# How x is loaded in a batched two-layer expert kernel: x(0) to x(3) in four loads from SyncE, x(4) to x(7) in one cast load from GpSimd

## The chip, the core and the metric

One core of a Trainium2 chip runs the kernel. The core has five engines: TensorE (PE) multiplies matrices, VectorE (DVE) and ScalarE (ACT) work on rows of data, GpSimd (POOL) and SyncE (SP) mostly issue transfers here. Sixteen DMA engines move data between HBM and the on-chip memory SBUF; matrix products come out in PSUM. Each program keeps its own order on each engine, and the engines meet through semaphores. The metric is the device time of one execution in microseconds (us), the median over runs.

## The reference

```python
n_experts, capacity, hidden, expert_hidden = 8, 256, 512, 2048
# x (8, 256, 512), w1 (8, 512, 2048), w2 (8, 2048, 512), all float32
h = np.matmul(x, w1)
h = np.maximum(h, 0)
return np.matmul(h, w2).astype(np.float32)
```

Eight independent experts, each with 256 rows of x, two matrix products and a ReLU between them. The weights are 67.1 MB in float32, x and the output 4.19 MB each.

## The kernel before

All sums are made in bfloat16 with float32 accumulation. The weights go from float32 in HBM to bfloat16 in SBUF inside the DMA (a cast load), which only GpSimd issues here. A weight slot w_sb holds one expert's w1 or w2 in bfloat16, and there are eight slots, so that two pairs of experts fit.

The experts run in four pairs p. For each pair GpSimd issues one load for both w1 and one for both w2 (4096 KB written each; for the last pair one load per expert, and its w2 in two pieces each). From the third pair on, such a load waits until PE has finished with the slots of two pairs earlier. GpSimd's loads go down one software ring, in order. SyncE counts their landings and hands PE a credit (t_w) for each.

x has to be transposed before it can be used. This is done for four experts at a time (a group g of two pairs): PE multiplies 128x128 blocks of the bfloat16 copy x_b with an identity into PSUM (ph), and ACT and DVE copy that into xt in the order in which the products need it (`untie`; who = 0 is ACT, who = 1 is DVE). Then for each expert PE makes h in four steps of 512 columns of w1, ACT and DVE write the ReLU of it in turns to ht, and PE makes the output from ht and w2 in PSUM (po). ACT and DVE copy it to x_f, which serves as the output's buffer too, and SyncE stores it: three pairs in one store of 3072 KB, which it issues once the first piece of the last expert's w2 has landed, and the last two experts in one store of 512 KB each.

Where x comes from before the change: x(0) and x(4 to 7) are loaded as float32 into x_f by SyncE, on its hardware ring, with rows of 4 KB and 16 KB per partition. Both stand inside the frame: the program up to `tc.close()`, at the end of which all engines meet at a barrier (line 96 in the profile) before any goes on. GpSimd loads x(1) and x(2 to 3) behind the frame as cast loads straight into x_b, ahead of all weights. ACT casts x(0) from x_f to x_b at the start; ACT and DVE cast one half each of x(4 to 7) during pair 0, when PE no longer reads the first group from x_b. SyncE waits for GpSimd's two x loads (line 145) and counts them for PE (t_x).

The lines that the change touches, by the profile's numbers: L91 the x loads, L145 SyncE's wait for them, L181 the casts, L192 and L196 the copies of `untie` for the first group, L287 the transposes.

Of the kernel before, what the change touches and what calls it, by code (L numbers as in the profile page):

```python
# [9 lines left out]
def kernel(  # L10
# [13 lines left out]
    nc = tc.nc  # L24
    P = 128
    bf = mybir.dt.bfloat16
# [3 lines left out]
    E, C, H = x.shape  # L30
    F = w1.shape[2]
    MT = C // P
    KT1 = H // P
# [4 lines left out]
    NG = E // 4  # L38
    J = 4 * MT
# [8 lines left out]
    def x_rows(es):  # L48

        flat = x[es].rearrange("e c k -> (e c k)")  # L50
        return flat.rearrange("(p f) -> p f", p=P)

    def sbuf(name, shape, dtype):
        return nc.alloc_sbuf_tensor(name, (P, *shape), dtype)

    def sem(name):
        return nc.alloc_semaphore(name)
# [1 line left out]


    x_f = sbuf("x_f", (NG, J, H), f32)
    x_b = sbuf("x_b", (J, H), bf)
    xt = sbuf("xt", (KT1, MT, 4 * P), bf)

    w_sb = sbuf("w_sb", (8, F * KT1), bf)
# [2 lines left out]
    ph = nc.alloc_psum_tensor("pt_h", (P, 2, FB, C), f32)  # L68
    po = nc.alloc_psum_tensor("pt_o", (P, 2 * MT, H), f32)

    s_x = [sem(f"s_x{i}") for i in range(4)]
    s_w = [sem(f"s_w{i}") for i in range(8)]
    s_cut = [sem(f"s_cut{b}") for b in range(2)]
    s_id = sem("s_id")
# [1 line left out]
    s_pe = sem("s_pe")  # L76
    t_x = sem("t_x")
# [5 lines left out]

    LOADS = [(0, 1), (4, 8), (1, 2), (2, 4)]

    def load_x(eng, to, i):
        a, b = LOADS[i]
        dst = to[:, MT * (a % 4):MT * ((b - 1) % 4 + 1), :].rearrange("p j k -> p (j k)")  # L90
        return eng.dma_start(dst, x_rows(slice(a, b))).then_inc(s_x[i], 16)  # L91

    for i in (0, 1):
        tc.no_tile_sem_insts.add(load_x(nc.sync, x_f[:, LOADS[i][0] // 4], i).ins.name)
    tc.close()
    tc.compile()  # L96

# [2 lines left out]
    at_t = lambda g, k: base(2 * g) - KT1 + k + 1  # L102
# [5 lines left out]


    pool = nc.gpsimd  # L110
    for i in (2, 3):
        load_x(pool, x_b, i)
    place = lambda p, i, b: 4 * i + 2 * (p % 2) + b
    landed = []
    for p, i in [(p, i) for p in range(NP) for i in range(2)]:
        joint = p < NP - 1
        for b in range(0, 2, 1 + joint):
            e, n = 2 * p + b, 1 + joint
            if p > 1:
                last = b + n - 1  # L120
                pool.wait_ge(s_pe, at_o(p - 2, last) if i else at_h(p - 2, last, NQ - 1))
            src = (w2_r if i else w1_r)[e:e + n].rearrange("e p f -> p e f")
            to = place(p, i, b)
            dst = w_sb[:, to:to + n]
# [15 lines left out]


    sp = nc.sync
    for i in (2, 3):
        sp.wait_ge(s_x[i], 16)
    sp.sem_inc(t_x, 1)  # L145
    times = [0] * len(s_w)
    for to, i, n in landed:
        times[to] += 1
# [21 lines left out]
    for who, (eng, copy, act) in enumerate((  # L170
        (nc.scalar, nc.scalar.copy, lambda o, i: nc.scalar.activation(o, i, relu)),  # L171
        (nc.vector, nc.vector.tensor_copy, nc.vector.tensor_relu),
    )):
        def cast(g):
            if g:
                eng.wait_ge(s_pe, at_t(g - 1, KT1 - 1))

            n = J // 2 if g else MT
            j0 = who * n
            eng.wait_ge(s_x[g], 16)  # L180
            copy(x_b[:, j0:j0 + n, :], x_f[:, g, j0:j0 + n, :]).then_inc(t_x, 1)  # L181

        def untie(g):


            for k in range(who, KT1, 2):
                eng.wait_ge(s_pe, at_t(g, k))
                src = ph[:, k // 2].bitcast(bf).rearrange("p a b -> p (a b)")
                src = src[:, k % 2 * J * P:(k % 2 + 1) * J * P]
                one, two = xt[:, k, :, :2 * P], xt[:, k, :, 2 * P:]  # L190
                if g == 0:
                    copy(  # L192
                        one.rearrange("p m (eh r) -> p m eh r", eh=4),
                        src[:, :4 * P].rearrange("p (eh r m) -> p m eh r", eh=4, m=MT),
                    )
                    last = copy(  # L196
                        two.rearrange("p m (e h r) -> p m h e r", e=2, h=2),
                        src[:, 4 * P:].rearrange("p (m h e r) -> p m h e r", m=MT, h=2, e=2),
                    )
                    continue  # L200
                for i in range(2):
                    part = src[:, 4 * P * i:4 * P * (i + 1)].rearrange(
                        "p (m h q) -> p m h q", m=MT, h=2
                    )
                    copy(  # L205
                        one.rearrange("p m (e h r l) -> p l m h e r", e=2, h=2, l=2)[:, i],
                        part[:, :, :, :P // 2].rearrange("p m h (e r) -> p m h e r", e=2),
                    )
                last = copy(  # L209
                    two.rearrange("p m (q l) -> p l m q", l=4),  # L210
                    src.rearrange("p (l m q) -> p l m q", l=4, m=MT)[:, :, :, P // 2:],
                )
            last.then_inc(t_h[who], 1)

        if who == 0:
            cast(0)
        for p in range(NP):
            if p % 2 == 0:
                untie(p // 2)
            for b in range(2):  # L220
                for q in range(who, NQ, 2):
                    eng.wait_ge(s_pe, at_h(p, b, q))
                    act(ht[:, b, FB * q:FB * (q + 1), :], ph[:, q % 2]).then_inc(t_h[who], 1)  # L223
            if p % 2 == 0 and p // 2 + 1 < NG:
                cast(p // 2 + 1)
            for b in range(2):
                eng.wait_ge(s_pe, at_o(p, b))
                if p == NP - 1:
                    copy(res(p)[:, MT * b + who, :], po[:, 2 * b + who, :]).then_inc(s_fin[b], 1)  # L229
                    continue  # L230
                for h in range(2):
                    src = po[P // 2 * h:P // 2 * (h + 1), 2 * b + who, :]
                    last = copy(res(p)[P // 2 * b:P // 2 * (b + 1), 2 * who + h, :], src)  # L233
                last.then_inc(t_o, 1)
# [5 lines left out]
    def take(s, n):  # L240
        pe.sem_inc(s, -n).wait_op(s, n, "sem-ge")  # L241

    def counter(name, step):

        r = nc.alloc_registers(name, engines=PE)
        nc.regs_mov(r, 0)
        add = lambda n: nc.regs_alu(r, r, n, op=mybir.AluOpType.add)
        now = lambda most: nc.snap(
            r, engines=PE, min_val=0, max_val=most, guaranteed_mod_val=0, out_of_modulus=step
        )  # L250
        return add, now

    def at(t, part, moved, dtype, *dims):

        n = part + moved
        dims_in = "abc"[:len(t.shape) - 1]
        line = t[:].rearrange(f"p {' '.join(dims_in)} -> p ({' '.join(dims_in)})")
        size = 2 if dtype == bf else 4
        last = sum(step * (num - 1) for step, num in dims) + 1
        got = line.bitcast(mybir.dt.uint8)[:, bass.ds(n, last * size)].bitcast(dtype)  # L260
        return bass.AP(got.tensor, got.offset, [got.ap[0], *([a, b] for a, b in dims)])

    def ready(places, **how):

        for place in places:
            pe.lower_ap(place, **how)
        return places

    def weights(places):
        return ready(places, for_matmul_weights=True)  # L270
# [2 lines left out]
        pe.sem_inc(s, 1)  # L273
    pe.sem_inc(t_o, 4)
    pe.wait_ge(s_id, 2)
    with nc.Fori(0, NG, engines=PE):
        take(t_x, 2)
        for t in t_h:
            take(t, 1)
        add_k, now_k = counter("r_k", 2)  # L280
        add_p, now_p = counter("r_p", 2 * J * P)
        with nc.Fori(0, KT1, engines=PE):
            k_at, p_at = now_k(2 * (KT1 - 1)), now_p(2 * J * P * (KT1 - 1))
            dsts = ready([at(ph, 2 * P * j, p_at, bf, [1, P]) for j in range(J)])
            srcs = weights([at(x_b, 2 * H * j, k_at, bf, [KT1, P]) for j in range(J)])
            for dst, src in zip(dsts, srcs):
                mm = pe.transpose(dst, src, identity[:])  # L287
            mm.then_inc(s_pe, 1)
            add_k(2)
            add_p(2 * J * P)  # L290
        W = 2 * F * KT1
        add_x, now_x = counter("r_x", 2 * P)
        add_w, now_w = counter("r_w", 4 * FB)
# [3 lines left out]
        with nc.Fori(0, 2, engines=PE):  # L297
            add_h, now_h = counter("r_h", 2 * C)
            add_o, now_o = counter("r_o", 4 * H * MT)
            with nc.Fori(0, 2, engines=PE):  # L300
                take(t_w, 1)
                with nc.Fori(0, NQ // 2, engines=PE):
                    x_at, w_at = now_x(6 * P), now_w(3 * W + 4 * FB)
                    cols = ready([
# [15 lines left out]
                    add_w(4 * FB)  # L320
                add_w(W - 2 * FB * NQ)
                add_x(2 * P)
# [3 lines left out]
            def second(kt0, n, turns=1):  # L326
                top = kt0 + n * (turns - 1)
                h_at, w_at = now_h(2 * C * (KT2 + top)), now_2(2 * H * (3 * KT2 + top))
                steps = [(kt, mt) for kt in range(n) for mt in range(MT)]
                cols = ready([at(w_sb, 4 * W + 2 * H * kt, w_at, bf, [1, H]) for kt in range(n)])  # L330
                rows = weights([
# [52 lines left out]
```

## Time and profile before

| what | value |
|---|---|
| time, median of 3 runs | 179.06 us (178.99 to 179.12) |
| time of the profiled execution | 179.03 us |
| its span, first to last instruction | 177.7 us |
| PE busy | 127.3 us (72%) |
| DVE, ACT, POOL busy | 36.1, 34.5, 9.4 us |
| software ring (GpSimd's loads) | 34.34 MB written, 91.0% of 16 DMA engines' span |
| hardware ring (SyncE's transfers) | 6.82 MB written, 9.3% |
| HBM read and written | 71.30 MB and 4.19 MB |

The execution took 1.3 us more than its span, which lies around the first and last instruction. The two rings' shares are the time that their packets took, divided by 16 engines' span; a share over 1 in a stretch comes about where packets of one DMA engine overlap, or where more of them start in the stretch than end in it. Bytes of a cast load are counted as written, and its reads are twice that.

### The profile page before, as it was taken

Reading aid. Unit: us, or ns where it says so; the run is one execution under the profiler, and the core shown is the slowest. Engines: PE = TensorE matmul, PEld = TensorE weight load, DVE = VectorE, ACT = ScalarE, POOL = GpSimd, SP = SyncE. Lnnn points to the kernel's source line nnn. Section 1 sums busy time; section 2 is a strip of 40 time slices with the busy share of each in tenths; the row PEclk is TensorE's granted clock in tenths of the full one; section 3 lists DMA queues with packets and bytes.
Section 4 is the critical chain, followed back from the end, with each engine's and each line's share of the span. In section 5 each row is a group of like instructions: output and inputs, shape, how many; then the busy total and the mean of one; then the engine's idle time right before and its main releaser. Section 6 shows DMA issues by size and latency. Waiting matters only on the chain. (4 is left out here: it accounts for less than half of the span.)

```text
span 177.7 us, 2366 instructions
## 1 busy us (share of the span) xinstructions
PE 127.3 (72%) x832; PEld 90.0 (51%) x832; DVE 36.1 (20%) x41; ACT 34.5 (19%) x43; POOL 9.4 (5%) x20
## 2 busy tenths in 40 slices
PE   0008000599929992899959993599999999999960
PEld 0007000499813440699814453489944489964420
DVE  0002100022340203022310309123222034420110
ACT  4104000024410202024200209022402042220110
POOL 3600000000010001001000202000000000000000
PEclk9999999999996998589969999579999999999997
DMA  6999999999999999999999999999999999999998
GB/s 236 376 240 210 236 203 210 236 203 210 236 207 207 236 207 207 236 210 203 236 210 203 236 210 203 236 218 195 236 218 195 236 218 203 209 224 204 291 435 341
DMA packets 3760, 41.16 MB, mean 232 GB/s; under 512 B 304, under 2 KB 304, under 8 KB 1200
## 3 DMA queue, kind: packets, MB, share of 16 engines
q0 software_dynamic: 2784, 34.34, 91.0%
q1 hardware_dynamic: 976, 6.82, 9.3%
HBM read 71.30 MB, written 4.19 MB: 425 GB/s over the span
## 5 line engine op out<-in xcount | busy, mean ns | idle before, releaser
L315 PE MATMUL pt_h<-xt,w_sb 128*128 x512 | 62.9, 290 | 24.4 <-PEq L241 24.4
L315 PEld LDWEIGHTS pt_h<-xt,w_sb 128*128 x512 | 59.3, 147 | 28.2 <-issue 25.2
L335 PE MATMUL pt_o<-w_sb,ht 128*128 x256 | 59.4, 394 | 6.1 <-PEq L241 5.8
L335 PEld LDWEIGHTS pt_o<-w_sb,ht 128*128 x256 | 25.5, 101 | 38.8 <-issue 12.2
L223 DVE TENSOR_SCALAR ht<-pt_h 128x1024 bf16<-128x1024 f32 x16 | 19.6, 1224 | 65.2 <-PE pt_h L315 65.2
L171 ACT ACTIVATE ht<-pt_h 128x1024 bf16<-128x1024 f32 x16 | 16.4, 1024 | 62.1 <-PE pt_h L315 62.1
L233 DVE COPY x_f<-pt_o 64x512 f32<-64x512 f32 x12 | 8.3, 689 | 42.1 <-PE pt_o L335 42.0
L233 ACT COPY x_f<-pt_o 64x512 f32<-64x512 f32 x12 | 7.0, 581 | 47.9 <-PE pt_o L335 47.8
L287 PE MATMUL pt_h<-identity,x_b 128*128 128x128 bf16 x64 | 5.6, 264 | 14.0 <-PEq L241 14.0
L287 PEld LDWEIGHTS pt_h<-identity,x_b 128*128 x64 | 5.1, 128 | 14.3 <-issue 14.0
L130 POOL DMA_DIRECT2D w_sb<-in_w_dram x8 | 5.4, 675 | 79.1 <-PE pt_h L315 60.6
L192 DVE COPY xt<-pt_h 128x512 bf16<-128x512 bf16 x2 | 1.4, 692 | 16.6 <-PE pt_h L287 16.6
L229 ACT COPY x_f<-pt_o 128x512 f32<-128x512 f32 x2 | 1.2, 586 | 14.4 <-PE pt_o L335 14.4
L229 DVE COPY x_f<-pt_o 128x512 f32<-128x512 f32 x2 | 1.4, 692 | 12.4 <-PE pt_o L335 12.4
L192 ACT COPY xt<-pt_h 128x512 bf16<-128x512 bf16 x2 | 1.2, 586 | 10.7 <-PE pt_h L287 10.7
L181 ACT CAST x_b<-x_f 128x1024 bf16<-128x1024 f32 (+1 forms) x2 | 2.9, 1468 | 0.3 <-DMA x_f<-in_x_dram 0.3
L209 ACT COPY xt<-pt_h 128x512 bf16<-128x512 bf16 x2 | 2.7, 1328 | 0.0
L209 DVE COPY xt<-pt_h 128x512 bf16<-128x512 bf16 x2 | 2.6, 1276 | 0.0
L127 POOL DMA_DIRECT2D w_sb<-in_w_dram x2 | 1.1, 531 | 16.3 <-PE pt_o L335 16.3
L181 ACT ACT_TABLE_LOAD x1 | 1.3, 1283 | 2.4 <-PEq L96 2.4
L205 ACT COPY xt<-pt_h 128x256 bf16<-128x256 bf16 x4 | 1.6, 487 | 0.0
L205 DVE COPY xt<-pt_h 128x256 bf16<-128x256 bf16 x4 | 1.6, 442 | 0.0
(11 smaller groups left out, 6.4 us busy)
## 6 DMA issues: line engine op xcount, KB each, us to landing
w_sb<-in_w_dram POOLq DMA_DIRECT2D x6, 4096.0 KB, 60.8
w_sb<-in_w_dram POOLq DMA_DIRECT2D x2, 2048.0 KB, 58.2
out_dram<-x_f SPq DMA_DIRECT2D x1, 3072.0 KB, 11.0
w_sb<-in_w_dram POOLq DMA_DIRECT2D x2, 1280.0 KB, 56.1
x_f<-in_x_dram SPq DMA_DIRECT2D x1, 2048.0 KB, 8.4
w_sb<-in_w_dram POOLq DMA_DIRECT2D x2, 768.0 KB, 59.2
out_dram<-x_f SPq DMA_DIRECT2D x2, 512.0 KB, 6.8
x_f<-in_x_dram SPq DMA_DIRECT2D x1, 512.0 KB, 3.2
```

The costliest lines, as they stand in the source:

```text
L130: pool.dma_start(dst, src).then_inc(s_w[to], 16)
L171: (nc.scalar, nc.scalar.copy, lambda o, i: nc.scalar.activation(o, i, relu)),
L181: copy(x_b[:, j0:j0 + n, :], x_f[:, g, j0:j0 + n, :]).then_inc(t_x, 1)
L192: copy(one.rearrange("p m (eh r) -> p m eh r", eh=4), src[:, :4 * P].rearrange("p (eh r m) -> p m eh r", eh=4, m=MT),)
L205: copy(one.rearrange("p m (e h r l) -> p l m h e r", e=2, h=2, l=2)[:, i], part[:, :, :, :P // 2].rearrange("p m h (e r) -> p m h e r", e=2),)
L209: last = copy(two.rearrange("p m (q l) -> p l m q", l=4), src.rearrange("p (l m q) -> p l m q", l=4, m=MT)[:, :, :, P // 2:],)
L223: act(ht[:, b, FB * q:FB * (q + 1), :], ph[:, q % 2]).then_inc(t_h[who], 1)
L229: copy(res(p)[:, MT * b + who, :], po[:, 2 * b + who, :]).then_inc(s_fin[b], 1)
L233: last = copy(res(p)[P // 2 * b:P // 2 * (b + 1), 2 * who + h, :], src)
L287: mm = pe.transpose(dst, src, identity[:])
L315: mm = pe.matmul(ph[:, q, i, :], row, cols[kt], start=(kt == 0), stop=(kt == KT1 - 1),)
L335: mm = pe.matmul(outs[mt], row, cols[kt], start=(kt0 + kt == 0), stop=(kt0 + kt == KT2 - 1),)
```

## The change

x(0) to x(3) are loaded by SyncE as float32 into x_f, one load of 512 KB per expert with rows of 4 KB per partition, each with its own semaphore. The first stands in the frame, the other three directly behind it. x(4 to 7) come in one cast load of GpSimd, its first, into a second half of x_b, which is twice as large now. The casts of the first group are split over ACT (x(0), x(2)) and DVE (x(1), x(3)); the casts of the second group and SyncE's wait for x are gone, and ACT and DVE count x(4 to 7) for PE after the ReLUs of pair 0. `untie` of the first group is one copy per 128 rows of K where it was two, since the rows of its four experts now all lie alike. PE's counter r_k goes on into the second half of x_b.

```diff
-    x_b = sbuf("x_b", (J, H), bf)
+    x_b = sbuf("x_b", (NG, J, H), bf)
...
-    LOADS = [(0, 1), (4, 8), (1, 2), (2, 4)]
-
-    def load_x(eng, to, i):
-        a, b = LOADS[i]
-        dst = to[:, MT * (a % 4):MT * ((b - 1) % 4 + 1), :].rearrange("p j k -> p (j k)")
-        return eng.dma_start(dst, x_rows(slice(a, b))).then_inc(s_x[i], 16)
-
-    for i in (0, 1):
-        tc.no_tile_sem_insts.add(load_x(nc.sync, x_f[:, LOADS[i][0] // 4], i).ins.name)
+    def load_x(e):
+        dst = x_f[:, 0, MT * e:MT * (e + 1), :].rearrange("p j k -> p (j k)")
+        return nc.sync.dma_start(dst, x_rows(slice(e, e + 1))).then_inc(s_x[e], 16)
+
+    EARLY = 1
+    for e in range(EARLY):
+        tc.no_tile_sem_insts.add(load_x(e).ins.name)
     tc.close()
     tc.compile()
+    for e in range(EARLY, 4):
+        load_x(e)
...
     pool = nc.gpsimd
-    for i in (2, 3):
-        load_x(pool, x_b, i)
+    pool.dma_start(
+        x_b[:, 1].rearrange("p j k -> p (j k)"), x_rows(slice(4, 8))
+    ).then_inc(s_x[4], 16)
...
-    for i in (2, 3):
-        sp.wait_ge(s_x[i], 16)
-    sp.sem_inc(t_x, 1)
...
-        def cast(g):
-            if g:
-                eng.wait_ge(s_pe, at_t(g - 1, KT1 - 1))
-
-            n = J // 2 if g else MT
-            j0 = who * n
-            eng.wait_ge(s_x[g], 16)
-            copy(x_b[:, j0:j0 + n, :], x_f[:, g, j0:j0 + n, :]).then_inc(t_x, 1)
+        def cast():
+            for e in range(who, 4, 2):
+                eng.wait_ge(s_x[e], 16)
+                at_e = slice(MT * e, MT * (e + 1))
+                last = copy(x_b[:, 0, at_e, :], x_f[:, 0, at_e, :])
+            last.then_inc(t_x, 1)
...
                 if g == 0:
-                    copy(
-                        one.rearrange("p m (eh r) -> p m eh r", eh=4),
-                        src[:, :4 * P].rearrange("p (eh r m) -> p m eh r", eh=4, m=MT),
-                    )
                     last = copy(
-                        two.rearrange("p m (e h r) -> p m h e r", e=2, h=2),
-                        src[:, 4 * P:].rearrange("p (m h e r) -> p m h e r", m=MT, h=2, e=2),
+                        xt[:, k].rearrange("p m (eh r) -> p m eh r", eh=J),
+                        src.rearrange("p (eh r m) -> p m eh r", eh=J, m=MT),
                     )
                     continue
...
-            if p % 2 == 0 and p // 2 + 1 < NG:
-                cast(p // 2 + 1)
+            if p == 0:
+                eng.wait_ge(s_x[4], 16)
+                eng.sem_inc(t_x, 1)
```

On SyncE the whole program is these rows, before (-) and after (+). L96 (L94 after) is the end of the frame; 128x4096 is x(4 to 7) in float32, 128x1024 one expert's x.

```order
-L379 UNCONDITIONAL_BRANCH
-L91 DMA x_f<-in_x_dram 128x1024
-L91 DMA x_f<-in_x_dram 128x4096
-L96 UNCONDITIONAL_BRANCH
-L157 DMA out_dram<-x_f 128x3x2048
-L163 DMA out_dram<-x_f 128x1024 x2
+L372 UNCONDITIONAL_BRANCH
+L88 DMA x_f<-in_x_dram 128x1024
+L94 UNCONDITIONAL_BRANCH
+L88 DMA x_f<-in_x_dram 128x1024 x3
+L155 DMA out_dram<-x_f 128x3x2048
+L161 DMA out_dram<-x_f 128x1024 x2
```

One of two loads has left the frame, and three now stand behind it. On GpSimd, from the end of the frame to the second weight load, it was this before:

```order
-L96 UNCONDITIONAL_BRANCH
-L91 DMA x_b<-in_x_dram 128x1024
-L91 DMA x_b<-in_x_dram 128x2048
-L130 DMA w_sb<-in_w_dram 128x2x8192 x2
-L133 MEMSET identity 128x128
```

and it is this after the change:

```order
+L94 UNCONDITIONAL_BRANCH
+L111 DMA x_b<-in_x_dram 128x4096
+L131 DMA w_sb<-in_w_dram 128x2x8192 x2
+L134 MEMSET identity 128x128
+L136 ISA
```

Two cast loads of x ahead of the weights have become one, which carries four experts where the two carried three.

## Rows read from the trace of the kernel before

**Rows 1.** Stretches of the span: engines' busy time, granted clock, DMA share, GB/s written.

```profile
core 0: us, PE busy (x) PEld busy (x) DVE busy (x) ACT busy (x) POOL busy (x), PEclk, DMA share, GB/s
0.00:1.75 1.75, 0.00 (x0) 0.00 (x0) 0.00 (x0) 0.00 (x0) 0.20 (x4) 1.00 0.00 0
1.75:2.25 0.50, 0.00 (x0) 0.00 (x0) 0.00 (x0) 0.00 (x0) 0.00 (x0) 1.00 0.71 213
...
3.25:3.75 0.50, 0.00 (x0) 0.00 (x0) 0.00 (x0) 0.42 (x1) 0.50 (x2) 1.00 1.34 500
3.75:7.00 3.25, 0.00 (x0) 0.00 (x0) 0.00 (x0) 1.04 (x1) 2.89 (x6) 1.00 0.97 403
...
9.00:12.00 3.00, 0.00 (x0) 0.00 (x0) 0.00 (x0) 0.00 (x0) 0.00 (x0) 1.00 1.08 214
12.00:31.50 19.50, 3.62 (x32) 3.24 (x32) 2.04 (x4) 2.15 (x4) 0.00 (x0) 1.00 1.04 222
31.50:112.50 81.00, 65.20 (x416) 45.08 (x416) 20.17 (x23) 18.28 (x23) 4.64 (x8) 0.91 1.02 217
112.50:163.00 50.50, 50.09 (x347) 38.20 (x348) 12.55 (x12) 10.52 (x12) 0.00 (x0) 0.95 1.02 216
163.00:177.00 14.00, 8.41 (x39) 3.42 (x36) 1.38 (x2) 1.17 (x2) 0.00 (x0) 0.96 0.99 355
```

**Rows 2.** The chain that ended last, in order of time: start, length, what.

```profile
112.87 0.04 issue
112.91 16.56 PE pt_h L315 x128
...
171.76 0.69 DVE x_f L229
```

**Rows 3.** SyncE's waits: in total, times, longest.

```profile
SPq L151 <- DMA w_sb<-in_w_dram: 147.3, 10, 19.4
...
SPq L96 <- PEq L96: 0.4, 2, 0.3
```

**Rows 4.** The first 36 us in order of time: start, length, what, idle before.

```profile
0.74 0.86 SPq L91 DMA_DIRECT2D x_f<-in_x_dram  x2
2.39 1.28 ACT L181 ACT_TABLE_LOAD   x1 [2.39 <-PEq L96]
2.88 1.19 POOL L91 DMA_DIRECT2D x_b<-in_x_dram  x2 [2.43 <-POOLq L96]
3.93 1.04 ACT L181 CAST x_b<-x_f 128x1024 bf16<-128x1024 f32 x1 [0.26 <-DMA x_f<-in_x_dram]
4.06 1.43 POOL L130 DMA_DIRECT2D w_sb<-in_w_dram  x2
...
18.24 0.41 DVE L196 COPY xt<-pt_h 128x512 bf16<-128x512 bf16 x1
...
33.11 3.09 PE L315 MATMUL pt_h<-xt,w_sb 128*128 x14 [15.52 <-PEq L241]
```

**Rows 5.** SyncE's two issues of x: duration ns min, median, max.

```profile
L91 SPq DMA_DIRECT2D x_f<-in_x_dram x2: 383/402/422, 0.7 to 1.2; - x2
```

**Rows 6.** DMA packets started at 2.20 to 3.15 us: packets, MB, share of 16 engines.

```profile
q1 hardware_dynamic: 97, 0.40, 103.1%
```

**Rows 7.** The same at 3.60 to 7.00 us.

```profile
q1 hardware_dynamic: 80, 1.31, 93.2%
```

**Rows 8.** The same at 7.05 to 7.50 us.

```profile
q1 hardware_dynamic: 9, 0.15, 77.9%
q0 software_dynamic: 12, 0.02, 28.9%
```

**Rows 9.** The same at 9.15 to 9.55 us.

```profile
q0 software_dynamic: 38, 0.08, 102.7%
```

**Rows 10.** The same at 10.25 to 11.75 us.

```profile
q0 software_dynamic: 76, 0.31, 102.6%
```

**Rows 11.** The same at 12.50 to 31.50 us, with the line of sizes.

```profile
DMA packets 255, 4.06 MB, mean 214 GB/s; under 512 B 7, under 2 KB 7, under 8 KB 7
...
q0 software_dynamic: 255, 4.06, 100.1%
```

**Rows 12.** Around the second group's casts, 44 to 54 us, in order of time.

```profile
47.85 1.89 ACT L181 CAST x_b<-x_f 128x2048 bf16<-128x2048 f32 x1
...
49.82 1.22 DVE L181 CAST x_b<-x_f 128x2048 bf16<-128x2048 f32 x1
...
52.07 2.26 PE L335 MATMUL pt_o<-w_sb,ht 128*128 x7 [3.43 <-PEq L241]
```

**Rows 13.** DMA issues: KB each, us from issue to landing.

```profile
x_f<-in_x_dram SPq DMA_DIRECT2D x1, 512.0 KB, 3.2
```

More of the change, by code (lines that the diff above doesn't have):

```diff
@@ L69 @@
     po = nc.alloc_psum_tensor("pt_o", (P, 2 * MT, H), f32)
-    s_x = [sem(f"s_x{i}") for i in range(4)]
+    s_x = [sem(f"s_x{i}") for i in range(5)]
     s_w = [sem(f"s_w{i}") for i in range(8)]
@@ L189, in untie @@
                 src = src[:, k % 2 * J * P:(k % 2 + 1) * J * P]
-                one, two = xt[:, k, :, :2 * P], xt[:, k, :, 2 * P:]
                 if g == 0:
-                    copy(
-                        one.rearrange("p m (eh r) -> p m eh r", eh=4),
-                        src[:, :4 * P].rearrange("p (eh r m) -> p m eh r", eh=4, m=MT),
-                    )
                     last = copy(
-                        two.rearrange("p m (e h r) -> p m h e r", e=2, h=2),
-                        src[:, 4 * P:].rearrange("p (m h e r) -> p m h e r", m=MT, h=2, e=2),
+                        xt[:, k].rearrange("p m (eh r) -> p m eh r", eh=J),
+                        src.rearrange("p (eh r m) -> p m eh r", eh=J, m=MT),
                     )
                     continue
+                one, two = xt[:, k, :, :2 * P], xt[:, k, :, 2 * P:]
                 for i in range(2):
@@ L213, in untie @@
             last.then_inc(t_h[who], 1)
-        if who == 0:
-            cast(0)
+        cast()
         for p in range(NP):
@@ L275 @@
     pe.wait_ge(s_id, 2)
+    add_k, now_k = counter("r_k", 2)
     with nc.Fori(0, NG, engines=PE):
@@ L279 @@
             take(t, 1)
-        add_k, now_k = counter("r_k", 2)
         add_p, now_p = counter("r_p", 2 * J * P)
         with nc.Fori(0, KT1, engines=PE):
-            k_at, p_at = now_k(2 * (KT1 - 1)), now_p(2 * J * P * (KT1 - 1))
+            k_at, p_at = now_k(2 * (J * H + KT1 - 1)), now_p(2 * J * P * (KT1 - 1))
             dsts = ready([at(ph, 2 * P * j, p_at, bf, [1, P]) for j in range(J)])
@@ L290 @@
             add_p(2 * J * P)
+        add_k(2 * (J * H - KT1))
         W = 2 * F * KT1
```

## The prediction

> **What bounds the kernel now.** I read the chain that ended last first. It says that PE worked without a break from 112.91 us to the last copy at 171.76 [rows 2], which looks like a kernel bound by PE. But a chain is only as good as its first link, so the next view is the waits. SyncE, which passes weight landings on to PE, stood for 147.3 us in ten waits for w_sb [rows 3]; PE's own row at 33.11 shows it idle for 15.52 us before the first products [rows 4]. The table of stretches then tells which side feeds which: from 12 us to 163 the DMA share is 1.02 to 1.04, and 0.99 in the last 14 us, while PE works 65.20 of 81.00 us in the middle [rows 1]. The DMA engines never run dry. The chain starts where a weight landing released PE, and PE's later work and the last stores hang on landings that come one behind another. So the end is: first packet at about 1.8 us (share 0 before 1.75, 0.71 in the half microsecond after [rows 1]), plus all the packets' time, plus any hole. A change in x moves the end by exactly what it does to the packets' time ahead of the weights and to holes there. The engines' work on x counts only if it gets later than 33.11 us, when the first products start.
>
> **The packets.** Each load of x spreads 128 rows over 16 DMA engines, 8 rows each, and each row here is one packet. The mean time of a packet is share x 16 x length of the stretch / packets:
> - float32 rows of 4 KB: 1.031 x 16 x 0.95 / 97 = 162 ns [rows 6];
> - float32 rows of 16 KB: 0.932 x 16 x 3.40 / 80 = 634 ns [rows 7];
> - cast rows that read 4 KB (x(1)): 1.027 x 16 x 0.40 / 38 = 173 ns [rows 9];
> - cast rows that read 8 KB (x(2 to 3)): 1.026 x 16 x 1.50 / 76 = 324 ns [rows 10];
> - cast rows that read 32 KB (weights): of 255 packets 7 are tiny, so 1.001 x 16 x 19.0 / 248 = 1227 ns [rows 11].
>
> All come to about 153 to 173 ns per 4 KB read, whichever ring they are on: what counts is bytes read, and those don't change. A cast row that reads 16 KB isn't in the trace. On a line from 324 ns at 8 KB to 1227 at 32 KB it takes 324 + 903 x 8 / 24 = 625 ns. Its bounds are half a weight row, 614, and two rows of 8 KB, 648.
>
> x(0) is common. Removed per DMA engine: 8 x 634 + 8 x 173 + 8 x 324 = 9.05 us. Added: 3 x 8 x 162 + 8 x 625 = 3.89 + 5.00 = 8.89 us. The sum is -0.16 us, with the bounds of the cast row -0.25 to +0.02. I take -0.16, since 16 KB lies between two measured sizes. That small cast packets overlapped more than others (share 1.08 between 9 and 12 us against 1.02 to 1.04 for the weights [rows 1]) could take some 0.1 us of this back.
>
> **The first hand-over, x(0) to x(1) on SyncE's ring.** Before, x(4 to 7) was issued right behind x(0), and the share was 1.34 from 3.25 to 3.75 [rows 1], so there was no hole. Now x(1) is issued behind the frame. When is that? SyncE issued from 0.74 to 1.60 [rows 4] and then waited only 0.4 us at the end of the frame [rows 3], while ACT's and POOL's waits there lasted to 2.39 and 2.43 [rows 4]: SyncE, the last to come, held the barrier. One issue less (422 ns at most [rows 5]) brings it 0.4 us forward. ACT's first instruction behind it stood at 2.39, so I put x(1)'s issue at about 2.0; if SyncE started as slowly as POOL (2.88), at 2.5. From issue to first packet x(0) took 1.8 - 0.74 = 1.06 us. x(1)'s packets can thus start at 3.1 to 3.5. x(0) keeps an engine busy for 8 x 0.162 = 1.3 us from 1.8 to 2.2 on, to 3.1 to 3.5. No hole, at most 0.4 us; I take 0. x(2) and x(3) follow at 0.42 us of issue each, against 1.3 us of packets, so the ring stays filled.
>
> Here a rule of the Trainium skill speaks against the change ("DMA: Bandwidth & Descriptors", section "Bandwidth"): batch transfers to at least 1 MiB, because a smaller one reaches a lower share of the peak; the page's table gives 341 GB/s at 1 MB against 425 at 16 MB. In this trace the 512 KB load with 4 KB rows ran at 162 ns per 4 KB, the 2048 KB load at 634 / 4 = 159: the size of the load is not seen as long as another stands behind it. By the fixed part of 2.0 us per load in the same page's section "Anatomy of one DMA" the three further loads would cost up to 6 us, an estimate. The trace shows such a part as latency (3.2 us to landing for 1.3 us of packets [rows 13]), and nothing in it shows that time taken from the engines.
>
> **The second hand-over, from SyncE's ring to GpSimd's.** This is the place with the least cover. POOL issued x(1) at 2.88 [rows 4], and the first software packets appear in the stretch from 7.05, with none from 3.60 to 7.00 [rows 7, 8]: 4.2 us later. Before, SyncE's ring held 1.3 + 5.1 us of packets, which is to 8.3 us: a cover of 1.3 us. Now it holds 4 x 1.3 = 5.2, which from 1.8 to 2.2 lasts to 7.0 to 7.4. The earlier barrier lets POOL issue at about 2.46; with the same 4.2 us its packets start at 6.7, a cover of some 0.3 to 0.7 us. I cost it at 0; from there on every 0.1 us later costs 0.1.
>
> **What costs nothing.** ACT and DVE cast two experts each (about 1.04 us each on ACT [rows 4]) behind landings that can't come later than the x packets end, about 12 us; the transposes start at about 14 as before, `untie` ends near 19, and PE waits for w1 until 33.11 [rows 4]. That is 14 us of cover for all edits of cast, transposes and `untie`, PE's counter too. The second group's casts (1.89 and 1.22 us) lay at 47.85 to 51.0, before PE started again at 52.07 for w2 [rows 12]; to take them away frees engines that were waiting. GpSimd issues one load less, ahead of weights that wait in the ring for tens of us anyway.
>
> **Sum.** 179.03 (the profiled execution's own time) - 0.16 = 178.87; the median of the runs was 0.03 higher, so 178.9 us. A measurement of this kernel can't tell less than about 0.2%, 0.36 us, from no change.
>
> **The rivals.**
> - *GpSimd's packets come late (slower).* The one cast load covers four experts, so its descriptors may take longer. For it: 4.2 us from issue to first packet is long and what fills it isn't seen; the cover falls from 1.3 us to some 0.5. Against it: POOL's issue row grows little from a small load to a weight load (1.19 us for two, 1.43 for two [rows 4]). If the first packet waited for the next issue too (0.72 us) on top of a start that isn't earlier (2.88 + 4.2), it comes at 7.8, a hole of 0.4 to 0.8 us; if the start grew with bytes, it would be near 9 and the hole 1.7. It decides from about 7.7 on; I price it at 0.6 to 1.0 net, 179.6 to 180.0. Chance 0.13.
> - *The start gets denser (faster).* From 3.75 to 7.00 the share was 0.97 on one ring alone, later 1.02 to 1.08 [rows 1]. If the two rings mix earlier and pack 5 to 8% tighter over these 3 to 5 us, that gives a further 0.25 to 0.4 us: 178.4 to 178.6. Against it: from 7.05 to 7.50 both rings together show 1.07 with few packets, no clear gain [rows 8]. Chance 0.18.
> - *Every load pays its fixed part.* If the 3.2 - 1.3 = 1.9 us of latency stood open on the ring ahead of each load, x(1) would run from about 5.2 to 6.5 and GpSimd would fill the rest from 6.7: a hole of about 2 us, 181. The seamless hand-over in rows 1 speaks against it. Chance 0.02. By the Trainium skill's rule above ("DMA: Bandwidth & Descriptors") this would be the outcome.
>
> **How the numbers follow.** No measurable change 0.67, faster 0.18, slower 0.15 (0.13 + 0.02). The likeliest case has its own range from 178.7 (bound -0.25 and a little denser) to 179.3 (bound +0.02 and the first hand-over's hole of 0.3). To leave out no more than 2 in 10, I reach into the middle of the faster case, 178.5, and to the near edge of the slower one, 179.6.
>
> **What would show it.** Right: hardware packets without a break from 1.8 us, the first software packets before 7.0, no stretch of the first 12 us with a DMA share well under 1 behind the start, the first products at about 32.9, and all later rows earlier by the same 0.1 to 0.2 us. SyncE's and POOL's first issues behind the frame near 2.0 and 2.5 would confirm the barrier. Wrong: a hole in the DMA share around 3.5 or around 7, with the first products late by as much; or an end that moves by something other than the first products do, which would mean that not the landings carry the end.

## The result, and the profile after

The changed kernel takes 180.98 us (median of 6 runs, 180.51 to 181.61) against 179.09 us before. The ratio is 1.0102, with a 95% interval of 1.0086 to 1.0118: slower by 1%, where 178.9 us and no measurable change was forecast. Its own spread is wider than before, 1.1 us against 0.57.

These are the first 46 us of the changed kernel in order of time (start, length, what, idle before and its releaser), which answer to [rows 4]:

```profile
0.74 2.45 SPq L88 DMA_DIRECT2D x_f<-in_x_dram  x4
1.92 1.28 ACT L176 ACT_TABLE_LOAD   x1 [1.92 <-PEq L94]
2.40 0.65 POOL L111 DMA_DIRECT2D x_b<-in_x_dram  x1 [1.96 <-POOLq L94]
...
11.81 0.69 DVE L176 CAST x_b<-x_f 128x1024 bf16<-128x1024 f32 x1 [11.81 <-DMA x_f<-in_x_dram]
22.25 1.04 ACT L176 CAST x_b<-x_f 128x1024 bf16<-128x1024 f32 x1 [17.19 <-DMA x_f<-in_x_dram]
34.42 0.69 DVE L176 CAST x_b<-x_f 128x1024 bf16<-128x1024 f32 x1 [21.92 <-DMA x_f<-in_x_dram]
36.20 3.37 PE L279 MATMUL pt_h<-identity,x_b 128*128 128x128 bf16 x32 [36.20 <-PEq L233]
...
42.19 4.06 PE L308 MATMUL pt_h<-xt,w_sb 128*128 x20 [2.62 <-PEq L233]
```

The barrier did come forward as forecast: ACT goes on at 1.92 (2.39 before), GpSimd issues at 2.40 (2.88 before). But x(1), x(2) and x(3) are cast only at 11.81, 22.25 and 34.42 us, and the first products start at 42.19 instead of 33.11 [rows 4].

The stretches of the changed kernel, with the columns of [rows 1]:

```profile
1.75:2.25 0.50, 0.00 (x0) 0.00 (x0) 0.00 (x0) 0.33 (x1) 0.00 (x0) 1.00 0.92 238
2.25:3.25 1.00, 0.00 (x0) 0.00 (x0) 0.00 (x0) 0.95 (x1) 0.85 (x2) 1.00 0.98 373
3.25:3.75 0.50, 0.00 (x0) 0.00 (x0) 0.00 (x0) 0.00 (x0) 0.50 (x1) 1.00 0.72 197
3.75:7.00 3.25, 0.00 (x0) 0.00 (x0) 0.00 (x0) 1.04 (x1) 2.68 (x6) 1.00 0.92 265
...
31.50:112.50 81.00, 65.00 (x448) 46.82 (x448) 20.42 (x23) 17.06 (x23) 4.63 (x8) 0.94 1.02 217
112.50:163.00 50.50, 47.34 (x334) 37.09 (x335) 14.31 (x15) 12.00 (x15) 0.00 (x0) 0.93 1.02 216
163.00:177.00 14.00, 11.04 (x52) 4.71 (x49) 1.38 (x2) 1.17 (x2) 0.00 (x0) 1.00 0.99 337
177.00:178.00 1.00, 0.00 (x0) 0.00 (x0) 0.00 (x0) 0.00 (x0) 0.00 (x0) 1.00 0.91 373
178.00:179.00 1.00, 0.00 (x0) 0.00 (x0) 0.00 (x0) 0.00 (x0) 0.00 (x0) 1.00 0.44 180
179.00:179.90 0.90, 0.00 (x0) 0.00 (x0) 0.00 (x0) 0.00 (x0) 0.00 (x0) 0.56 0.07 27
```

Two things are to be seen. There is a hole: the share is 0.72 where it was 1.34 before, at the first hand-over (3.25 to 3.75 us [rows 1]), the point at which x(0)'s rows end and those of the next load begin. And the end has a tail: the DMA share goes down over three microseconds, 0.91, 0.44, 0.07. Some engines finish well before others. In the kernel before, the end was steep:

```profile
176.00:177.00 1.00, 0.00 (x0) 0.00 (x0) 0.00 (x0) 0.00 (x0) 0.00 (x0) 0.50 0.91 373
177.00:177.70 0.70, 0.00 (x0) 0.00 (x0) 0.00 (x0) 0.00 (x0) 0.00 (x0) 0.50 0.08 29
```

The same lag can be read where the second weight load lands. Each of 16 engines closes a load with one tiny completion packet, and SyncE's credit waits for all 16. Before, the line of packet sizes for 50.70 to 51.25 us holds all of them ("under 512 B"):

```profile
DMA packets 32, 0.26 MB, mean 477 GB/s; under 512 B 16, under 2 KB 16, under 8 KB 16
```

In the changed kernel 51.50 to 52.00 us holds 5, and even the two microseconds from 51.50 to 53.50 hold 15:

```profile
DMA packets 14, 0.15 MB, mean 295 GB/s; under 512 B 5, under 2 KB 5, under 8 KB 5
...
DMA packets 42, 0.44 MB, mean 221 GB/s; under 512 B 15, under 2 KB 15, under 8 KB 15
```

The times at which the trace counts each load's semaphore say the same of all of them: the 16 landings of one weight load lie 0.45 to 0.52 us apart before, and 1.9 to 2.1 us in the changed kernel, from the first weight load on; those of the last store, 0.47 and 1.94 us.

So the DMA engines got out of step in the first microseconds and never came back into step: each has its fixed share of the rows of every load, and the queue never lets them wait for each other. The end of the kernel is the end of the slowest engine. The profiled executions differ by 2.2 us (span 179.9 against 177.7).

### The profile page after: what moved, and what is told of

It is laid out like the page before. It is cut to its first block, busy times and chain, and to the rows that moved or that the text cites. A ratio compares the mean times of both kernels' runs of the same rounds, so it can differ in the third digit from the quotient of the medians.

```text
span 179.9 us, 2364 instructions
## 1 busy us (share of the span) xinstructions
PE 123.4 (69%) x832; PEld 88.6 (49%) x832; DVE 36.8 (20%) x40; ACT 33.6 (19%) x41; POOL 8.9 (5%) x19
## 5 line engine op out<-in xcount | busy, mean ns | idle before, releaser
L308 PE MATMUL pt_h<-xt,w_sb 128*128 x512 | 60.9, 285 | 9.6 <-PEq L233 9.6
L308 PEld LDWEIGHTS pt_h<-xt,w_sb 128*128 x512 | 58.3, 146 | 12.4 <-issue 10.4
L328 PE MATMUL pt_o<-w_sb,ht 128*128 x256 | 57.9, 389 | 4.8 <-PEq L233 4.8
L176 DVE CAST x_b<-x_f 128x1024 bf16<-128x1024 f32 x2 | 1.4, 694 | 33.7 <-DMA x_f<-in_x_dram 33.7
L176 ACT CAST x_b<-x_f 128x1024 bf16<-128x1024 f32 x2 | 2.1, 1044 | 18.0 <-DMA x_f<-in_x_dram 18.0
L187 ACT COPY xt<-pt_h 128x1024 bf16<-128x1024 bf16 x2 | 2.0, 1013 | 14.7 <-PE pt_h L279 14.7
L187 DVE COPY xt<-pt_h 128x1024 bf16<-128x1024 bf16 x2 | 2.4, 1224 | 3.3 <-PE pt_h L279 3.3
L201 ACT COPY xt<-pt_h 128x512 bf16<-128x512 bf16 x2 | 2.7, 1330 | 0.0
L201 DVE COPY xt<-pt_h 128x512 bf16<-128x512 bf16 x2 | 2.5, 1274 | 0.0
```

The costliest lines, as they stand in the source:

```text
L176: last = copy(x_b[:, 0, at_e, :], x_f[:, 0, at_e, :])
L187: last = copy(xt[:, k].rearrange("p m (eh r) -> p m eh r", eh=J), src.rearrange("p (eh r m) -> p m eh r", eh=J, m=MT),)
L201: last = copy(two.rearrange("p m (q l) -> p l m q", l=4), src.rearrange("p (l m q) -> p l m q", l=4, m=MT)[:, :, :, P // 2:],)
L308: mm = pe.matmul(ph[:, q, i, :], row, cols[kt], start=(kt == 0), stop=(kt == KT1 - 1),)
L328: mm = pe.matmul(outs[mt], row, cols[kt], start=(kt0 + kt == 0), stop=(kt0 + kt == KT2 - 1),)
```

## The experiments

Three theories of what put the engines out of step. **S**: an engine that has moved its 8 rows of x(0) before rows of x(1), issued behind the frame, reach it, runs dry, and stands still for longer than the rows take to come. **R**: SyncE's ring can't feed rows of 4 KB as fast as engines move them. **G**: GpSimd's issues hold up SyncE's ring. Each timed ratio below is against runs of the kernel before on the same chip, with its 95% interval. The trace doesn't name the engine of a packet, so that some engines stand while others move is read from the DMA share.

**One part alone: the second load behind the frame.** The kernel before, with x(4 to 7) issued after `tc.close()`:

```diff
-    for i in (0, 1):
-        tc.no_tile_sem_insts.add(load_x(nc.sync, x_f[:, LOADS[i][0] // 4], i).ins.name)
+    tc.no_tile_sem_insts.add(load_x(nc.sync, x_f[:, 0], 0).ins.name)
     tc.close()
     tc.compile()
+    load_x(nc.sync, x_f[:, 1], 1)
```

> The kernel before with one thing changed: the load of x(4 to 7), rows of 16 KB, is issued behind the frame, not in it. Theory S (what costs is that the second load reaches the engines only when x(0) has run out): a hole between 3.3 and 4.3 us as in the changed kernel, engines out of step from there on, first weight load landing 0.3 to 1 us later on the slowest engine, 179.4 to 180.2. Theory R (4 KB rows behind one another are what the ring can't feed): rows of 16 KB, so no change, 179.0 to 179.2. Theory G (GpSimd's issues, now at 2.4 us, hold up the hardware ring): slow packets between 3.4 and 5 us, 179.3 to 180.5, without the hole at 3.3.

Measured: 180.89 us, ratio 1.0103 (1.0068 to 1.0137). This one edit gives the whole loss of the change, with rows of 16 KB. R falls as the main cause. The size is above every range given: S had 180.2 at most, G 180.5. The stretch from 3 to 7 us, first before, then here, has the share 1.05 and then 0.83:

```profile
3.00:7.00 4.00, 0.00 (x0) 0.00 (x0) 0.00 (x0) 1.72 (x2) 3.64 (x7) 1.00 1.05 423
3.00:7.00 4.00, 0.00 (x0) 0.00 (x0) 0.00 (x0) 1.24 (x2) 3.64 (x8) 1.00 0.83 281
```

This run also shows that the loss doesn't come from the late first products of the changed kernel. Here they start at 35.02, only 1.9 us later than before, and the loss is the same:

```profile
35.02 3.39 PE L315 MATMUL pt_h<-xt,w_sb 128*128 x15 [15.69 <-PEq L241]
```

**The same place, in the changed kernel.** x(1) to x(3) in one issue of 384 rows of 4 KB, once behind the frame (shown) and once in it; the casts wait for this one load:

```diff
-    for e in range(EARLY, 4):
-        load_x(e)
+    nc.sync.dma_start(
+        x_f[:, 0, MT:, :].rearrange("p (e j) k -> p e (j k)", j=MT),
+        x[1:4].rearrange("e (p j) k -> p e (j k)", p=P),
+    ).then_inc(s_x[1], 16)
```

> The changed kernel, but x(1) to x(3) come in one issue behind the frame, 384 rows of 4 KB. Theory S: the hole at 3.3 to 4.5 us stays as in the changed kernel, since this issue stands where x(1)'s stood; after that nothing to wait for: 179.8 to 180.8. Theory R: the hole goes on to 6.5 us, 180.5 to 181.5. Theory G: slow packets from 3.4 to 5 us as in the changed kernel, 180 to 181.3.

> The changed kernel with x(1) to x(3) in one issue of 384 rows of 4 KB, issued in the frame. It differs from the kernel with that one issue behind the frame (181.39 us) by the place alone. Theory S (engines that run dry before the second load's rows reach them stand still for 1 to 1.7 us): rows are there before x(0) ends, no hole, 179.0 to 179.6. Theory G (what costs is GpSimd's descriptor work beside rows of 4 KB): GpSimd issues 0.45 us later, hole and slow packets move by as much, 180.3 to 181.4.

Behind the frame: 181.39 us, ratio 1.0129 (1.0112 to 1.0146). In the frame: 179.45 us, 1.0015 (1.0006 to 1.0024). The two kernels differ by where one instruction is issued. The packets started from 3.50 to 4.50 us, rows of 4 KB and a few completions (packets, MB, share of 16 engines), behind the frame:

```profile
q1 hardware_dynamic: 45, 0.16, 49.6%
```

and in the frame:

```profile
q1 hardware_dynamic: 84, 0.32, 96.4%
```

Behind the frame half of the engines' time is lost over this microsecond, and its share from 3.50 to 5.00 is still 0.53. In the frame the same rows of 4 KB keep the engines busy. In the frame the time lies in S's range and far from G's. Behind it, it is 0.6 us above S's range; by its size alone that number would suit R (180.5 to 181.5), which the run before has ruled out. So S has the place right, and priced the hole too low.

**GpSimd later.** The identity is made ahead of GpSimd's first load, so that it issues later; with the second load behind the frame, and, as the control, with it in the frame as before (the lines put in, shortened; the later making of the identity is gone):

```diff
     pool = nc.gpsimd
+    pool.memset(identity[:], 0.0).then_inc(s_id, 1)
+    pool.wait_ge(s_id, 1)
+    pool.affine_select(...).then_inc(s_id, 1)
     for i in (2, 3):
         load_x(pool, x_b, i)
```

> The kernel before with the load of x(4 to 7) behind the frame, and the making of the identity ahead of GpSimd's first load, which so is issued at about 3.4 us (2.40 without that, 2.88 in the kernel before). Theory S: the hole at 3.5 us stays, 180.0 to 181. Theory G: GpSimd no longer works while SyncE's ring hands over, 179.0 to 179.5. If both are needed: a hole under 1 us instead of 1.1 to 1.7, 179.5 to 180.2.

> The kernel before with the making of the identity ahead of GpSimd's first load (issue at about 3.8 us, 2.88 without). Control for the run beside it. The software ring's first packets come 0.9 us later, at about 8.0, and SyncE's ring has packets until 8.3 to 9: all theories 179.0 to 179.3; above 179.5 the second hand-over has no such cover.

Behind the frame: 181.67 us, 1.0132 (1.0114 to 1.0149), slower than S's range; in the frame 179.14 us, 0.9998 (0.9989 to 1.0007). GpSimd issued at 2.84 and 3.31 us, half a microsecond earlier than I had expected, but in the first case as late as in the kernel before (2.88 [rows 4]). So its earlier issue isn't what costs, and in the control a later issue costs nothing. GpSimd was still at work during the hand-over, so this run doesn't show what its work there adds.

**A load behind the frame that doesn't find dry engines.** The kernel before with SyncE's two loads swapped: x(4 to 7) in the frame, x(0) behind it.

```diff
-    for i in (0, 1):
-        tc.no_tile_sem_insts.add(load_x(nc.sync, x_f[:, LOADS[i][0] // 4], i).ins.name)
+    tc.no_tile_sem_insts.add(load_x(nc.sync, x_f[:, 1], 1).ins.name)
     tc.close()
     tc.compile()
+    load_x(nc.sync, x_f[:, 0], 0)
```

> The kernel before with its two SyncE loads in the other order: x(4 to 7), rows of 16 KB and 5 us of packets, in the frame, and x(0) behind it, issued at 1.9 us. A load stands behind the frame here too, but no engine is near the end of its first load when it comes. Theory S (engines that run dry before the next rows are there stand still): no hole between 3 and 7 us; what is left is the start with rows of 16 KB, which cost 0.45 us in the run with one 16 KB-row load: 179.2 to 179.8. Theory F (a load issued behind the frame costs by itself, by the earlier barrier or by its place beside GpSimd's issues): 180.5 to 181.7, as with the loads the other way round.

Measured: 179.78 us, 1.0034 (1.0021 to 1.0047), at the upper end of S's range and far from the other. From 3 to 7 us the engines take 375 GB/s, against 281 with the loads the other way round (the share leaves out long packets begun before 3 us):

```profile
3.00:7.00 4.00, 0.00 (x0) 0.00 (x0) 0.00 (x0) 0.20 (x1) 3.64 (x8) 1.00 0.90 375
```

The place behind the frame costs nothing like 1% when the first load covers the engines for 5 us. What is left resembles the run with one 16 KB-row load below; it was not taken apart further.

**How many loads in the frame.** `EARLY` of 2 and of 4, else the changed kernel:

```diff
-    EARLY = 1
+    EARLY = 2
```

> Loads of x(0) and x(1) stand in the frame, x(2) and x(3) behind it. Theory S: x(1) is issued at 1.13 us and follows x(0) without a hole; x(2), issued at about 2.4, is due on an engine only at 4.4: share near 1.0, 179.0 (178.7 to 179.5). Theory R: the hole stays, 180 to 181.6. Theory G: as R, the hole from about 3.5 us, 179.5 to 181.5.

> All four 4 KB-row loads of x(0) to x(3) stand in the frame. Theory S (an engine is through with its 8 packets of x(0) before rows of x(1), issued only behind the frame at 1.91 us, reach it): issued from 0.74 on without a break, the DMA share stays near 1.0 from 2.25 to 7 us, the 16 parts of the first weight load land within 0.5 us of each other again, time 179.0 (178.7 to 179.4). Theory R (the hardware ring can't supply 4 KB rows as fast as engines move them, whenever they are issued): the hole of 3.25 to 6.25 us stays, share 0.7 to 0.9, landings spread over 1 to 2 us, 180 to 181.6. Theory G (GpSimd's issues from 2.40 us on hold up the hardware ring): GpSimd starts 1.3 us later, so the hole starts after 3.7 us, 179.5 to 181.

With two: 179.67 us, 1.0028 (1.0014 to 1.0042), 0.2 us above S's range. With four: 180.22 us, 1.0050 (1.0036 to 1.0064), 0.8 us above it. Both lie in G's ranges. With four the hole at the first hand-over is gone (share 1.03 from 3.50 to 4.50 us), but a new slow stretch stands at 4.25 to 5.25, just after GpSimd's first issue at 3.83.

**The same with GpSimd later still.** Four in the frame, and GpSimd behind the identity, or waiting for x(1):

```diff
     pool = nc.gpsimd
+    pool.wait_ge(s_x[1], 16)
```

> All four 4 KB-row loads in the frame, and the identity made ahead of GpSimd's first load, so issued at about 4.8 us (3.83 without that). Theory G: the hole and the slow packets that stood at 4.5 to 5.5 us move to 5.4 to 6.5 or vanish; theory S: they stay at x(1)'s hand-over to x(2), 4.5 to 5.5. Time 180 to 181 in either case, since the software ring starts later than SyncE's ring lasts.

> All four 4 KB-row loads in the frame, and GpSimd waits for x(1) to land (about 5 us) before its first load, so that it issues nothing in the first 5 us. Theory G: no hole and no packet over 300 ns between 3 and 6 us, x(0) to x(3) each land within 0.6 us; the second hand-over then starves (software ring from 9 us on), some 1.5 to 2.5 us late, 180.5 to 182. Theory R: share under 0.9 from 4.5 to 5.5 us as with all four in the frame and GpSimd free. Theory S alone predicts no hole here and would have predicted none there.

Measured: 180.53 us, 1.0075 (1.0057 to 1.0094), and 181.54 us (one run). The stretch from 4.25 to 5.25 us, first with GpSimd's first issue at 3.83, then at 4.27, then at 5.63:

```profile
4.25:5.25 1.00, 0.00 (x0) 0.00 (x0) 0.00 (x0) 0.99 (x2) 1.00 (x3) 1.00 0.83 254
```

```profile
4.25:5.25 1.00, 0.00 (x0) 0.00 (x0) 0.00 (x0) 0.99 (x2) 0.98 (x2) 1.00 1.04 401
```

```profile
4.25:5.25 1.00, 0.00 (x0) 0.00 (x0) 0.00 (x0) 0.99 (x2) 0.00 (x0) 1.00 1.06 389
```

The slow stretch of x's loads vanishes when GpSimd issues later, seen in one profile each. So GpSimd may be a smaller, second cause, but that isn't shown. With its issue at 4.27 it is at work for 0.98 us of this very stretch, and the ring still moves 401 GB/s; and no slow stretch follows the later issues (share 0.99 and 0.98 from 5.25 to 6.25). Nor does the time get better, since both kernels lose again later, at the second hand-over (share 0.98 and 0.96 from 7.20 to 9.20, against 1.15 with GpSimd at 3.83), where SyncE's ring ends before the software ring is in full flow.

**GpSimd silent.** It waits for x(3):

```diff
     pool = nc.gpsimd
+    pool.wait_ge(s_x[3], 16)
```

> GpSimd waits for x(3) to land before its first load; nothing else changes. Theory G: the four loads of the hardware ring run without a hole, share near 1.0 from 2.25 to 6.8 us, x(3) lands at about 7.3. Theories S and R: the hole between 3.25 and 6.25 stays with the software ring silent, x(3) lands at 8 to 9. In either case the software ring starts some 4 us after x(3) has landed, so the time is 183 to 186.

Measured: 184.44 us (one run), as all expected. The hole at the first hand-over is there with the software ring silent:

```profile
3.50:4.50 1.00, 0.00 (x0) 0.00 (x0) 0.00 (x0) 0.32 (x1) 0.00 (x0) 1.00 0.57 184
4.50:5.50 1.00, 0.00 (x0) 0.00 (x0) 0.00 (x0) 0.72 (x1) 0.00 (x0) 1.00 1.01 410
```

It is over by 4.50. That is S and not G, and a shorter hole than with GpSimd at work (0.63 and 0.87 in the same two stretches of the changed kernel). How much of the 1.9 us would be left without GpSimd's work, this run can't say, since its time is that of the wait.

**Other ways to load x(0) to x(3).** In one issue with rows of 4 KB, or one load with rows of 16 KB, both in the frame. The second puts the output rows of experts 2 and 3 in another order; its transfers and products are the same. The lines put in:

```diff
+        dst = x_f[:, 0].rearrange("p (e j) k -> p e (j k)", j=MT)
+        src = x[0:4].rearrange("e (p j) k -> p e (j k)", p=P)
+        return nc.sync.dma_start(dst, src).then_inc(s_x[e], 16)
```

```diff
+        dst = x_f[:, 0].rearrange("p j k -> p (j k)")
+        return nc.sync.dma_start(dst, x_rows(slice(0, 4))).then_inc(s_x[e], 16)
```

> x(0) to x(3) come in one issue in the frame, 512 rows of 4 KB; x(4 to 7) by GpSimd as in the changed kernel. Theory S: one issue at 0.74 us, no hand-over, no hole, 178.9 to 179.4. Theory R: engines wait for rows all through 2 to 7 us, share 0.7 to 0.9, 180 to 181.5. Theory G: slow packets some 1 to 2 us after GpSimd's first issue, that is 3.5 to 5 us, engines out of step by about 1 us, 179.5 to 180.5.

> x(0) to x(3) come in one load with rows of 16 KB, issued in the frame, in the layout of the second group (its untie copies serve both groups); everything else as in the changed kernel. Theories S and R: an engine has 5.1 us of packets from one issue, no hole, landings within 0.5 us; packets by the measured times 8 x 634 + 8 x 625 against 10.3 us of the kernel before, so 178.8 (178.5 to 179.1). Theory G: also a hole while GpSimd issues (2.4 to 5 us), 179.5 to 181.

Measured: 179.66 us, 1.0030 (1.0020 to 1.0040), and 179.55 us, 1.0020 (1.0011 to 1.0030). S missed both, the first by 0.26 us above its range and the second by 0.75 us from its 178.8 (R's too). Both times lie at the low end of G's ranges (from 179.5), but what G gives as the reason isn't there: they are slow before GpSimd issues (2.46 and 2.40). Neither has a hand-over on SyncE's ring; both begin slowly. The first 1.5 us of packets in the kernel before, then with one issue of 4 KB rows, then with one load of 16 KB rows (bytes count where their packet starts):

```profile
1.75:3.25 1.50, 0.00 (x0) 0.00 (x0) 0.00 (x0) 0.86 (x1) 0.37 (x1) 1.00 0.96 358
```

```profile
1.75:3.25 1.50, 0.00 (x0) 0.00 (x0) 0.00 (x0) 1.28 (x1) 0.79 (x2) 1.00 0.91 175
```

```profile
1.75:3.25 1.50, 0.00 (x0) 0.00 (x0) 0.00 (x0) 1.28 (x1) 0.85 (x2) 1.00 1.13 240
```

358 GB/s against 175 and 240, with the engines counted as busy: the packets themselves are slow. With one issue of 4 KB rows, 16 packets start from 1.75 to 2.25 us:

```profile
q1 hardware_dynamic: 16, 0.07, 136.9%
```

That is 1.369 x 16 x 0.50 / 16 = 0.68 us each, where such a row took 0.16 us in the kernel before [rows 6]. So the plain sum of packets, which had them faster than before, doesn't hold at a start. Why is open.

## Why the prediction was wrong

- **The step that failed** is the first hand-over: "No hole, at most 0.4 us; I take 0." The issue came when forecast (behind a barrier that was 0.47 us earlier), but I let an engine that had run dry start again as soon as rows were there, and put the cost at 0. The runs show a hole that lasts to 4.5 us with GpSimd silent and to about 5 with it at work. In the changed kernel a second one follows, with a share of 0.68 from 5.00 to 5.70 us, before the first software packet; with x(1) to x(3) in one issue there is none (1.06 from 5.25 to 6.25), and the loss is as large. Placing the second load in the frame or behind it moves the time by 181.39 - 179.45 = 1.9 us in one pair and by 180.89 - 179.04 = 1.85 us in the other, which is the loss of the change, 1.9 us.
- **A second step made it look small**: the end "moves by exactly what it does to the packets' time ahead of the weights and to holes there" was worked out as a mean over 16 engines. The mean loss at the hand-over is small (share 0.74 from 3.25 to 4.75 in the changed kernel, 0.4 us); the loss of the slowest engine is what lands last, and it runs through to the stores. Of the last store's 16 landings the first comes 0.8 us later than before (177.94 against 177.18), the last 2.2 us (179.88 against 177.65). The Trainium skill has the rule behind it ("DMA: Bandwidth & Descriptors", section "Why a DMA increments its semaphore by 16 and not by 1"): the engines of one DMA finish independently and the semaphore counts them. The trace agrees: 5 of 16 completions in the first half microsecond of a landing, 15 in two.
- **The sum of packets, -0.16 us,** had the wrong sign. The profile of the changed kernel has these shares of its 179.9 us:

```profile
q0 software_dynamic: 2640, 34.60, 90.6%
q1 hardware_dynamic: 1264, 6.29, 8.9%
```

  Together they are 99.5% or 179.0 us, against (91.0% + 9.3%) x 177.7 = 178.2 us before. So the packets took some 0.8 us more in the mean, a slow packet's waiting counted with them, and this is part of the lag. The sum was too good for a start: the run with one 16 KB-row load was to save 0.27 us by it and lost 0.45.
- **"What costs nothing"** gave the right cost by a wrong route. I had x landed by about 12 us. SyncE's rows that were late met the weights on the same engines: from 13 to 31 us the changed kernel starts these packets:

```profile
q0 software_dynamic: 224, 3.64, 94.6%
q1 hardware_dynamic: 99, 0.34, 5.1%
```

  On the engines that are late, each row of x waits for a weight row of 32 KB, 1.2 us, before the next can go, so that x(3) is cast only at 34.42. The Trainium skill has the rule for it (same page, section "Queues, rings and completion order"): a DMA engine takes its rings in turn, packet by packet. The trace agrees: x(3) is cast 12.2 us after x(2), where 8 rows of x and 8 weight rows in turn make 8 x (0.162 + 1.227) = 11.1 us. The prediction asked when the two rings hand over, and not what a late row of x meets there: the weights behind the cast load. The first products were 9.1 us late for it and the cover of 14 us was used up, but the second pair's products start at 74.06 us against 71.78 before: 2.28 us later, the lag of the DMA engines and no more. The prediction's sign that not the landings carry the end (an end that moves by something other than the first products do) so came up for another reason: it was x that was late.
- **The second hand-over** held: the first software packets came before 7.0 us (24 of them between 5.70 and 7.00). The 4.2 us from issue to first packet that I carried over were not a property of GpSimd's path: with its issue at 5.63 us the first ones come between 7.1 and 7.4.
- **The rivals**: the outcome lay on the slower side (0.15), near the third rival's place but at none of the three mechanisms. The late software packets were not the cause; the fixed part of each load, at 181, had the right place and, by luck, the right size, but not the mechanism: with all three further loads in one issue behind the frame the loss is the same (181.39), and with that issue in the frame it is nearly gone. So it isn't a price per load. The 2.0 us that the prediction takes from the Trainium skill ("DMA: Bandwidth & Descriptors", section "Anatomy of one DMA") is stated there for GpSimd's path, and these loads are SyncE's.

What stays open: why a dry engine stands for up to 1.5 us although rows for its neighbours flow; whether GpSimd's issues lengthen this, and how; and why a start with more or longer rows is slow.

## What to carry to other kernels

Where transfers bound a kernel, the next load has to be issued well before the first engine has finished its rows of the last one: here 8 rows of 4 KB, 1.3 us, were too short a cover for an issue at 1.91 us and enough for one at 1.18, and a first load of 5 us was enough for the later place. Read the landing of a load as 16 landings, and price a hole by the slowest engine and not by the mean share. No variant tried beats the kernel before; the nearest is its control with GpSimd later (0.9998).

## What the runs showed of the hardware that was not expected

- Engines that get out of step at 3 to 5 us are still out of step at 179 us, by some 2 us; no later load brings them together as long as the rings never run empty. Where GpSimd's first load started on idle engines only after x(3), at 184.44 us, the share is still 1.04 from 181 to 182 us and 0.29 in the last 1.1, and the 16 landings of the last store lie 0.67 us apart: the cost there was the wait, and the tail is short.
- The first packets on idle engines can be slow, and slower with a larger load: one issue of 512 rows of 4 KB moved 175 GB/s in the first 1.5 us, one of 128 rows of 16 KB 240, x(0) with x(4 to 7) behind it 358.
- GpSimd's ring started sooner where SyncE's ring held less: first packets 4.2 us after the issue at 2.88 [rows 4, 8], under 1.8 us after an issue at 5.63, and 1.3 us after one at 10.19, when SyncE's ring was empty. That the one is due to the other isn't shown.
